# Squares summed on TensorE in the norms, and the query and key norm moved to the two large PSUM tiles, in a two-block transformer kernel

## The chip, the cores and the metric

The kernel runs on one core of a Trainium2 chip. A core has five engines that run side by side and meet at semaphores: PE (TensorE, matrix products into PSUM), DVE (VectorE), ACT (ScalarE), POOL (GpSimd) and SP (SyncE, which here only issues transfers). The metric is device time in microseconds (us) of one execution, the median over the runs. Lower is better.

## The reference, cut to what matters

Two blocks follow each other on 256 tokens of width 1024, all in float32. The first has one layer: stick-breaking attention, a retention branch, and a mixture of 16 experts. The second has two layers, each with half a feed-forward network, a mixing part (neighbourhood attention, pooled means, attention with grouped queries) and another half network, on 256 latent tokens `x` and 256 context tokens `ctx`. The second layer does the context only as far as the latent tokens need it.

```python
def _rmsnorm(x, g):
    y = x32 * lax.rsqrt(jnp.mean(x32 * x32, axis=-1, keepdims=True) + EPS)
    return (y * g.astype(jnp.float32)).astype(x.dtype)
...
h_x = _half_ffn(h_x, norm_g[l, 0], ..., ffn1_up[l], ffn1_down[l])
a_x = _modulate(_rmsnorm(h_x, norm_g[l, 1]), ...)
p_x = a_x @ w_in[l]
q_c = _rope_2d(_rmsnorm(p_x[..., OFF_C_Q:OFF_C_K].reshape(...), q_norm_g[l]), ang_row, ang_col)
k_c = _rope_2d(_rmsnorm(p_x[..., OFF_C_K:OFF_C_V].reshape(...), k_norm_g[l]), ang_row, ang_col)
o_b = _pool_mix(p_x[..., OFF_B_U:OFF_C_Q], pool_w[l], pool_scale[l])
o_c = _gqa_blocks(q_c, ...)
h_x = h_x + mod_x[:, :, 5] * (jnp.concatenate([o_a, o_b, o_c], axis=-1) @ w_out[l])
h_x = _half_ffn(h_x, norm_g[l, 2], ..., ffn2_up[l], ffn2_down[l])
...
return _rmsnorm(h_x, final_g)
```

The change touches two computations: the sum of squares over 1024 features that every `_rmsnorm` needs, and the norm and rotation of the queries and keys, 64 features a head.

## The kernel before, in words

**Products.** Activations lie feature by token: `self.h` holds eight tiles of 128 features by 256 tokens, once for the latent half (`v` = 0) and once for the context half (`v` = 1). A float32 product is made of three (`gemm`, lines 250 to 252): both factors are split into a high and a low part, and high by high, low by high and high by low add up in one PSUM tile. Weights arrive by DMA as `raw`, ACT copies the high part into `w` (L228) and DVE subtracts the low part (L237), for all of the kernel's weights.

**Sum of squares.** A norm's squares are made while the layer before is still writing `h`. `square` takes two feature tiles at once: ACT squares them into a tile `sq`, one engine adds the two halves (L351) and adds the result to `sqa` (L352). That engine is POOL, for the last pair DVE. Where the layer before ends with single tiles (the down projections of the networks), `square1` does the last two feature tiles singly: ACT squares, POOL adds the seventh and DVE the eighth to `sqa` (L357). Then `rstd` sums `sqa` over its 128 partitions by a product with a column of ones, one for each 128 tokens (L323, tile `ss`), DVE makes the reciprocal root of it (`nv`, `nr_y`, L325 and L288 to L303), `spread` turns it into rows again on PE (`rb`, L315), and `apply` multiplies (`xt`, L333) and splits into `xH` and `xL` (L338 and L339), which the next projections read. There are twelve such norms, and each has its two products on PE.

**Queries and keys.** `qk_norm` is a generator, whose steps the mixing part calls between the products of its other projections (`pj`). It waits for three steps, then does five tiles `t`, the keys (4) first and four of queries. For each, `widen` spreads the reciprocal roots (`qrw`, L1543 on ACT, L1545 on DVE for the keys), `scale` transposes them on PE into `qrp` (L1533) and multiplies on DVE (L1535), and a step later `turn` does the rotation: a product `qpp` on PE (L1549), and three DVE operations, of which the first (`qra`, L1551) reads `qpp`. In the first layer a tile has 512 tokens (`full`), in the second 256 for the queries.

**Buffers.** Two rings of PSUM matter. `mm` has four tiles of 128 x 512 and serves the projections `pj`, and before the change `qrp` and `qpp` too. `a2` has two tiles of 128 x 2 x 512, for the attention scores `as` and the sums `qss`. In SBUF, the ring `s` of seven tiles (`s512`) serves `sq`, `xt`, `qrw`, `qra`, and the tiles of `pool_sums` on POOL (`pla`, `plb`, `plc`, `pld`, `py`, L1710 to L1723). A new tile of a ring waits until the last reader of its place is done. A scheduler fixes the order of each engine's instructions when the program is built; each engine then runs its list in order.

**The end.** After the last down projection (`pd`, added into `h` at L698) comes the last norm: `finish` scales `h` by the final gains (L1743), transposes it on PE (`op`, L1747), multiplies by the norm (L1751 on DVE, L1753 on ACT) and stores.

Of the kernel before, what the change touches and what calls it, by code (L numbers as in the profile page):

```python
# [12 lines left out]
ALU = mybir.AluOpType  # L13
# [5 lines left out]
S = 256  # L19
# [151 lines left out]
class Builder:  # L171
# [147 lines left out]
    def rstd(self, sq):  # L319
        nc = self.nc  # L320
        ss = self.nps("ss")
        for t in range(2):
            nc.tensor.matmul(ss[:, t:t + 1], sq[0][:, t * 128:(t + 1) * 128], self.ones[:, 0:1], start=True, stop=True)  # L323
        m = self.small([128, 2], "nv")
        nc.vector.tensor_scalar(m, ss[:, :2], 1.0 / D, EPS, ALU.mult, ALU.add)  # L325
        return self.rsqrt(m, 2, "nr")
# [14 lines left out]
    def square(self, v, i, sq, last=3):  # L341
        nc = self.nc
        t = self.s512("sq")
        hs = self.h[:, 2 * i:2 * i + 2, v * S:(v + 1) * S]
        nc.scalar.activation(t.rearrange("p (j t) -> p j t", j=2), hs, AF.Square)
        e = nc.vector if i == last else nc.gpsimd
        if not sq:
            sq.append(self.scr.tile([128, S], F32, tag="sqa", name="sqa", bufs=2))
            e.tensor_tensor(sq[0], t[:, :S], t[:, S:], ALU.add)
        else:  # L350
            e.tensor_tensor(t[:, :S], t[:, :S], t[:, S:], ALU.add)  # L351
            e.tensor_tensor(sq[0], sq[0], t[:, :S], ALU.add)  # L352

    def square1(self, v, j, sq, e):
        t = self.s512("sq")[:, :S]
        self.nc.scalar.activation(t, self.h[:, j, v * S:(v + 1) * S], AF.Square)
        e.tensor_tensor(sq[0], sq[0], t, ALU.add)  # L357

    def normed(self, l, n, v, sq):
        for _ in range(NORM_LAG[v][0 if n < 2 else 2]):  # L360
# [226 lines left out]
    def ffn(self, l, n, up, dn, vs, side, pace, after):  # L587
        nc = self.nc
        self.raw_n, self.raws = 0, 7
        half = lambda v: slice(v * S, (v + 1) * S)  # L590
        with ExitStack() as st:
# [9 lines left out]
            for pi, nf in enumerate(PARTS):  # L601
# [3 lines left out]
                full = slice(0, N)  # L605
                off_up = OFF_512 if N == 512 else OFF_258 if late else OFF_256
                off_dn = OFF_512 if N == 512 else OFF_256
                for c in range(nf // 2):
# [4 lines left out]
                    for i in range(2):  # L613
# [20 lines left out]
                        for z in range(0, len(todo), 2):  # L634
                            pa, pb = todo[z][1][:, full], todo[z + 1][1][:, full]
                            if late:
                                p = pabs.pop(0)
                                ab = self.small([128, 2], "ab")
                                s = self.s512("fs").rearrange("p (a t) -> p a t", a=2)
# [4 lines left out]
                                t = self.s512("ft")[:, full]  # L644
                                nc.vector.scalar_tensor_tensor(t, s[:, 1], ab[:, 1:2], s[:, 0], ALU.add, ALU.mult)
                            else:
                                s = self.s512("fs")[:, full]
                                nc.scalar.activation(s, pa, AF.Silu)  # L648
                                t = self.s512("ft")[:, full]
# [9 lines left out]
                if pi < len(PARTS) - 1:  # L659
                    for dc in range(4):  # L660
                        v = self.rows(dn, f0 * 128, nf, dc * 256, 256)
                        for i in range(2):
                            w = self.split_w(v[:, :, i * 128:(i + 1) * 128], off_dn)
                            p = self.mm("pd")
                            self.gemm(p[:, full], w, lambda f: hid[f])
                            for v2 in range(N // S):
                                self.residual(p[:, half(v2)], 2 * dc + i, l, n, v2)
                        for _ in range(pace[1] if N == full_n else 1):
                            next(side, None)
                else:  # L670
                    ws = [self.split_w(self.rows(dn, f0 * 128, nf, dc * 256, 256), OFF_256) for dc in range(4)]
                    for v in sorted(vs):
                        sq = []
                        for d in range(KD):
                            cs = slice(d % 2 * 128, d % 2 * 128 + 128)
                            w = [z[:, :, cs] for z in ws[d // 2]]
                            p = self.mm("pd")[:, :S]
                            self.gemm(p, w, lambda f: (hid[f][0][:, half(v)], hid[f][1][:, half(v)]))
                            self.residual(p, d, l, n, v)
                            next(side, None)  # L680
                            self.advance()
                            if d >= 6:
                                self.square1(v, d, sq, nc.vector if d == 7 else nc.gpsimd)
                            elif d % 2:
                                self.square(v, d // 2, sq)
                        for _ in side:
                            pass
                        self.settle()
                        if after is not None:
                            self.pending = self.normed(*after, v, sq)  # L690
                        else:
                            self.sq = sq
# [817 lines left out]
    def qk_norm(self, l, ss, qc, ks, g8, cos, sin, full, P):  # L1510
        nc = self.nc
        kH, kL = ks
        hs = [slice(0, 64), slice(64, 128)]
        NX = 512 if full else 256
        sv = ss[:, :40].rearrange("p (t c a) -> p t c a", t=5, a=2)
        v = P.tile([128, 5, 4, 2], F32, name="qv")
        if not full:
            nc.vector.memset(v, 1.0)
            nc.vector.tensor_scalar(v[:, :4, :2], sv[:, :4, :2], 1.0 / 64, EPS, ALU.mult, ALU.add)
            nc.vector.tensor_scalar(v[:, 4], sv[:, 4], 1.0 / 64, EPS, ALU.mult, ALU.add)  # L1520
        else:
            nc.vector.tensor_scalar(v, sv, 1.0 / 64, EPS, ALU.mult, ALU.add)
        r = self.rsqrt(v.rearrange("p t c a -> p (t c a)"), 40, "qr")
        for _ in range(3):
            yield True
        r = r.rearrange("p (t c a) -> p t c a", t=5, a=2)

        def scale(t):
            n = 512 if t == 4 else NX
            rp = self.mm("qrp")[:, :n]  # L1530
            wide = wides.pop(t)
            for c in range(n // 128):
                nc.tensor.transpose(rp[:, c * 128:(c + 1) * 128], wide[:, c * 128:(c + 1) * 128], self.ident)  # L1533
            g = self.vec("kn", l) if t == 4 else g8
            nc.vector.scalar_tensor_tensor(qc[:, t, :n], qc[:, t, :n], g, rp, ALU.mult, ALU.mult)  # L1535

        def widen(t):
            n = 512 if t == 4 else NX
            wides[t] = self.s512("qrw")[:, :n]
            o = wides[t].rearrange("p (c a d) -> p c a d", a=2, d=64)  # L1540
            i = r[:, t, :n // 128, :, None].to_broadcast([128, n // 128, 2, 64])
            if t < 4:
                nc.scalar.activation(o, i, AF.Copy)  # L1543
            else:
                nc.vector.tensor_copy(o, i)  # L1545

        def turn(t):
            pp = self.mm("qpp")[:, :256]
            nc.tensor.matmul(pp, self.perm2, qc[:, t, :256], start=True, stop=True)  # L1549
            a_ = self.s512("qra")[:, :256]  # L1550
            nc.vector.tensor_tensor(a_, pp, sin, ALU.mult)  # L1551
            nc.vector.tensor_tensor(qc[:, t, :256], qc[:, t, :256], cos, ALU.mult)
            nc.vector.tensor_tensor(qc[:, t, :256], a_, qc[:, t, :256], ALU.add)
            if t == 4:
                for kv in range(2):
                    i = qc[hs[kv], 4, :]
                    for a in range(2):
                        nc.scalar.activation(kH[hs[a], kv, :], i, AF.Copy)
                for kv in range(2):
                    i = qc[hs[kv], 4, :]  # L1560
                    for a in range(2):
                        nc.vector.tensor_tensor(kL[hs[a], kv, :], i, kH[hs[kv], kv, :].bitcast(F32), ALU.subtract)

        last, wides = None, {}
        widen(4)
        widen(0)
        for t in (4, 0, 1, 2, 3, None):
            if t is not None:
                scale(t)
                if t in (4, 0, 1):  # L1570
                    widen((t + 2) % 5 if t < 4 else 1)
                yield True
            if last is not None:
                turn(last)
                yield True
            last = t
# [223 lines left out]
```

## Time and profile before

| | |
|---|---|
| Runs of the kernel before | 2236.61, 2228.87, 2228.74 us; median 2228.87 us |
| The profiled execution | 2224.97 us, with a span of 2223.1 us in the trace |
| PE busy | 2154.5 us, 97% of the span |
| DVE, ACT, POOL busy | 1438.2 us (65%), 816.9 us (37%), 178.0 us (8%) |
| Granted clock of PE, mean | 0.993 of full |

The times of the trace (the rows below) are those of the profiled execution, counted from the start of its span. A start such as 910.30 is a place on that clock. "Idle before" is how long an engine stood before an instruction, and the name behind the arrow is what ended that. A product of float32 operands without the split (as `ss`) shows as two rows of PE in the trace.

### The profile page before, as it was taken

How to read it: one execution, taken by the hardware profiler on the slowest of the kernel's cores; microseconds unless marked ns; L12 is line 12 of the kernel's file. 1: busy time of each engine (PE TensorE's matmuls, PEld its weight loads, DVE VectorE, ACT ScalarE, POOL GpSimd, SP SyncE). 2: the span in 40 equal slices, each digit the busy share in tenths (PEclk: the TensorE clock that was granted, in tenths of full speed). 3: DMA queues.
4: the chain of work that ended last, by engine and by line, in shares of the span. 5: the costliest groups of instructions: out<-in, count | busy, mean ns of one | idle time of the engine just before them, and what ended most of it. 6: DMA issues, size and time to landing. Idle time of an engine off the chain costs nothing.

```text
span 2223.1 us, 32479 instructions
## 1 busy us (share of the span) xinstructions
PE 2154.5 (97%) x13295; PEld 1775.8 (80%) x13295; DVE 1438.2 (65%) x2516; ACT 816.9 (37%) x1256; POOL 178.0 (8%) x204
## 2 busy tenths in 40 slices
PE   8999999997999999989999999999999999999998
PEld 8789975543688888977888877788878888879998
DVE  5656852221489787766678777638874345877776
ACT  5564531110233322347642222224222223575443
POOL 0200100000000000340120000000000003312000
PEclk9999999999999999999999999999999999999999
DMA  8674769998946655320236555333553212317551
GB/s 260 209 259 127 253 246 336 374 384 352 352 153 217 231 181 165 87 67 29 95 118 204 185 181 189 128 125 115 197 185 104 90 58 78 109 34 234 185 181 47
DMA packets 285461, 395.91 MB, mean 178 GB/s; under 512 B 18156, under 2 KB 220540, under 8 KB 285180
## 3 DMA queue, kind: packets, MB, share of 16 engines
q1 hardware_dynamic: 284288, 392.33, 52.2%
q8 instruction: 106, 1.74, 0.3%
q0 software_dynamic: 576, 1.18, 0.2%
q14 instruction: 47, 0.39, 0.1%
q10 hardware_dynamic: 444, 0.27, 0.0%
HBM read 392.71 MB, written 1.05 MB: 177 GB/s over the span
## 4 chain that ended last, share of the span: by engine, by line
PE 68%; DVE 6%; ACT 1%; POOL 1%; issue 1%; ACTq 0%; DVEq 0%; POOLq 0%
PE pab L250 12%; PE pab L251 12%; PE pab L252 12%; PE pd L250 6%; PE pd L251 6%; PE pd L252 6%; PE pj L250 1%; PE pj L251 1%; PE pj L252 1%; PE egu L1162 1%; PE aT L1652 1%; PE as L1623 1%; PE ao L1669 1%; DVE w L237 1%; PE ada_ps L531 1%; PE po L250 1%
## 5 line engine op out<-in xcount | busy, mean ns | idle before, releaser
L228 ACT ACTIVATE w<-raw 128x1024 fp32r<-128x1024 f32 (+2 forms) x432 | 425.5, 990 | 664.6 <-PE pd L252 238.6
L237 DVE TENSOR_TENSOR w<-raw,w 128x1024 fp32r<-128x1024 f32 (+2 forms) x422 | 481.2, 1150 | 181.3 <-ACT w L228 179.4
L251 PE MATMUL pab<-xL,w 128*128 128x512 f32 (+2 forms) x1600 | 545.0, 341 | 2.6 <-DVE xL L339 1.6
L250 PE MATMUL pab<-xH,w 128*128 128x512 f32 (+2 forms) x1600 | 545.2, 341 | 0.2
L252 PE MATMUL pab<-xH,w 128*128 128x512 f32 (+2 forms) x1600 | 544.1, 341 | 0.0
L250 PEld LDWEIGHTS pab<-xH,w 128*128 128x128 f32 x1600 | 301.7, 189 | 48.8 <-issue 8.2
L251 PEld LDWEIGHTS pab<-xL,w 128*128 128x128 f32 x1600 | 301.8, 189 | 42.3 <-issue 4.1
L252 PEld LDWEIGHTS pab<-xH,w 128*128 128x128 f32 x1600 | 301.8, 189 | 37.9 <-issue 4.1
L549 DVE SCALAR_TENSOR_TENSOR acc<-raw,sT,acc 128x512 f32<-128x512 f32 x420 | 284.8, 745 | 0.0
L250 PE MATMUL pd<-hH,w 128*128 128x512 f32 (+1 forms) x800 | 264.9, 333 | 0.5 <-ACT hH L241 0.2
L251 PE MATMUL pd<-hL,w 128*128 128x512 f32 (+1 forms) x800 | 264.5, 332 | 0.0
L252 PE MATMUL pd<-hH,w 128*128 128x512 f32 (+1 forms) x800 | 264.0, 331 | 0.0
L250 PE MATMUL pj<-xH,w 128*128 128x256 f32 (+1 forms) x816 | 248.5, 306 | 10.9 <-DVE qra L1551 5.2
L251 PE MATMUL pj<-xL,w 128*128 128x256 f32 (+1 forms) x816 | 243.3, 298 | 1.4 <-DVE xL L339 0.5
L252 PE MATMUL pj<-xH,w 128*128 128x256 f32 (+1 forms) x816 | 242.6, 298 | 0.5 <-DVE w L237 0.5
L250 PEld LDWEIGHTS pj<-xH,w 128*128 128x128 f32 x816 | 155.3, 191 | 26.5 <-DVE qra L1551 6.0
L250 PEld LDWEIGHTS pd<-hH,w 128*128 128x128 f32 x800 | 149.6, 188 | 20.4 <-ACT fs L648 3.4
L698 DVE SCALAR_TENSOR_TENSOR h<-pd,gmod,h 128x256 f32<-128x256 f32 x224 | 100.7, 478 | 99.0 <-PE pd L252 98.6
L252 PEld LDWEIGHTS pd<-hH,w 128*128 128x128 f32 x800 | 150.0, 188 | 16.8 <-issue 1.7
L251 PEld LDWEIGHTS pd<-hL,w 128*128 128x128 f32 x800 | 150.4, 188 | 15.4 <-DVE hL L242 0.3
L251 PEld LDWEIGHTS pj<-xL,w 128*128 128x128 f32 x816 | 155.7, 191 | 7.1 <-DVE xL L339 1.9
L252 PEld LDWEIGHTS pj<-xH,w 128*128 128x128 f32 x816 | 155.5, 191 | 5.5 <-DVE w L237 0.8
(388 smaller groups left out, 2457.5 us busy)
## 6 DMA issues: line engine op xcount, KB each, us to landing
raw<-ffn_up SPq DMA_DIRECT2D x94, 1024.0 KB, 5.3
raw<-w_ada SPq DMA_DIRECT2D x72, 1024.0 KB, 5.3
raw<-ffn_down SPq DMA_DIRECT2D x52, 768.0 KB, 4.7
raw<-w_in SPq DMA_DIRECT2D x32, 1024.0 KB, 5.7
raw<-w_exp_gate SPq DMA_DIRECT2D x32, 1024.0 KB, 10.0
raw<-w_exp_up SPq DMA_DIRECT2D x32, 1024.0 KB, 9.7
raw<-w_exp_down SPq DMA_DIRECT2D x32, 1024.0 KB, 8.7
raw<-w_gate SPq DMA_DIRECT2D x8, 1024.0 KB, 5.6
```

What stands on the lines that cost most here:

```text
L228: self.nc.scalar.activation(wh, v, AF.Copy)
L237: self.nc.vector.tensor_tensor(wl, v, wh.bitcast(F32), ALU.subtract)
L250: mm(o, wH[:, k, :], aH, start=(first and k == 0), stop=False)
L251: mm(o, wH[:, k, :], aL, start=False, stop=False)
L252: mm(o, wL[:, k, :], aH, start=False, stop=(last and k == n - 1))
L531: mm(ps[g * 32:(g + 1) * 32, :], self.unit[:, 31 - r:63 - r], acc[v], start=(u < 2), stop=(u > 3))
L549: ins = V.scalar_tensor_tensor(acc[v], w[:, g, :], s, acc[v], ALU.mult, ALU.add)
L698: self.nc.vector.scalar_tensor_tensor(hs, p, self.gmod[:, l, n, d, v:v + 1], hs, ALU.mult, ALU.add)
L1162: mm(pr[a * 64:a * 64 + 64, m, :], xg[p // 2][:, q * 2 + kk, es[a] % 4 * 64:es[a] % 4 * 64 + 64], w[:, a, kk * 512:(kk + 1) * 512], start= ...
L1623: mm(o[:, c], qs, x[i][:, c], start=(i == 0 and not (near and c.start == 0)), stop=(i == 1))
L1652: nc.tensor.transpose(T[:, j * 128:(j + 1) * 128], e[:, a, j * 128:(j + 1) * 128], self.ident)
L1669: mm(o[hs[a], qt * 128:(qt + 1) * 128], v[:, j, vo[a]:vo[a] + 64], pT[:, a, j, :], start=(j == 0), stop=(j == 3))
```

## The change

The diff, whole:

```diff
@@ rstd
         for t in range(2):
-            nc.tensor.matmul(ss[:, t:t + 1], sq[0][:, t * 128:(t + 1) * 128], self.ones[:, 0:1], start=True, stop=True)
+            for i, s in enumerate(sq):
+                nc.tensor.matmul(ss[:, t:t + 1], s[:, t * 128:(t + 1) * 128], self.ones[:, 0:1],
+                                 start=(i == 0), stop=(i == len(sq) - 1))
@@ square
-        e = nc.vector if i == last else nc.gpsimd
-        if not sq:
+        e = nc.gpsimd
+        if i == last:
+            sq.extend((t[:, :S], t[:, S:]))
+        elif not sq:
             sq.append(self.scr.tile([128, S], F32, tag="sqa", name="sqa", bufs=2))
             e.tensor_tensor(sq[0], t[:, :S], t[:, S:], ALU.add)
         else:
             e.tensor_tensor(t[:, :S], t[:, :S], t[:, S:], ALU.add)
             e.tensor_tensor(sq[0], sq[0], t[:, :S], ALU.add)
 
-    def square1(self, v, j, sq, e):
+    def square1(self, v, j, sq):
         t = self.s512("sq")[:, :S]
         self.nc.scalar.activation(t, self.h[:, j, v * S:(v + 1) * S], AF.Square)
-        e.tensor_tensor(sq[0], sq[0], t, ALU.add)
+        sq.append(t)
@@ ffn
-                                self.square1(v, d, sq, nc.vector if d == 7 else nc.gpsimd)
+                                self.square1(v, d, sq)
@@ qk_norm
-        for _ in range(3):
+        for _ in range(3 if full else 5):
             yield True
@@ scale
             n = 512 if t == 4 else NX
-            rp = self.mm("qrp")[:, :n]
+            both[t] = self.a2("qrp")
+            rp = both[t][:, 0, :n]
@@ turn
-            pp = self.mm("qpp")[:, :256]
+            pp = both.pop(t)[:, 1, :256]
@@ qk_norm
-        last, wides = None, {}
+        last, wides, both = None, {}, {}
```

In words: the last two squared feature tiles of a norm are no longer added to `sqa`, and `ss` is the sum of three products for each 128 tokens in place of one. In the program built from it PE has 48 matrix products more (12 norms by 4), DVE 17 additions fewer and POOL 7 fewer. The query and key norm's two PSUM tiles are now the two halves of one tile of the ring `a2`, and in the second layer it begins two steps later.

The scheduler orders the instructions anew. Three places, with the rows of each engine's order. `sqc` also names the constant that holds the ones and the identity. What stands in brackets is what the instruction may have to wait for; line numbers beyond L320 are one to five higher after the change.

On PE at the program's end, from the last down projection to the last transposes, before:

```order
L252 MATMUL pd<-hH,w 128x256
L323 MATMUL ss<-sqc,sqa 128x1 [waits DVE_49]
L323 MATMUL ss<-sqc,sqa 128x1
L1747 MATMUL op<-sqc,h 128x128 x11
L1747 MATMUL op<-sqc,h 128x128 [waits DVE_49] x2
L1747 MATMUL op<-sqc,h 128x128 x3
```

and after:

```order
L252 MATMUL pd<-hH,w 128x256
L324 MATMUL ss<-sqc,sqa 128x1 [waits DVE_49,Pool_49]
L324 MATMUL ss<-sqc,sq 128x1 [waits Activation_49]
L1752 MATMUL op<-sqc,h 128x128 [waits DVE_49]
L1752 MATMUL op<-sqc,h 128x128 x3
L1752 MATMUL op<-sqc,h 128x128 [waits DVE_49]
L1752 MATMUL op<-sqc,h 128x128 x3
L1752 MATMUL op<-sqc,h 128x128 [waits DVE_49]
L324 MATMUL ss<-sqc,sq 128x1 [waits Activation_49]
L324 MATMUL ss<-sqc,sqa 128x1
L324 MATMUL ss<-sqc,sq 128x1 x2
```

Two products of the sum and nine transposes of `op` have moved ahead of the product that reads the last square.

On DVE in the second layer's query and key norm, from the last step of its reciprocal root to the rotation of the keys, before:

```order
L237 TENSOR_TENSOR w<-raw,w 128x1024 [waits DMAHW1_49,PE_49,Activation_49]
L308 SCALAR_TENSOR_TENSOR qr_y<-qr_a,qr_y 128x40 [waits DVE_49]
L1545 COPY qrw<-qr_y 128x512 [waits DVE_49]
L1535 SCALAR_TENSOR_TENSOR qc<-qc,vT,qrp 128x512 [waits PE_49]
L1535 SCALAR_TENSOR_TENSOR qc<-qc,g_16744,qrp 128x256 [waits PE_49]
L237 TENSOR_TENSOR w<-raw,w 128x1024 [waits Activation_49]
L1551 TENSOR_TENSOR qra<-qpp,rot_16707 128x256 [waits DMASW6_49,PE_49,Pool_49]
```

and after:

```order
L237 TENSOR_TENSOR w<-raw,w 128x1024 [waits DMAHW1_49,PE_49,Activation_49]
L308 SCALAR_TENSOR_TENSOR qr_y<-qr_a,qr_y 128x40 [waits DVE_49]
L237 TENSOR_TENSOR w<-raw,w 128x1024 [waits PE_49,Activation_49]
L1550 COPY qrw<-qr_y 128x512 [waits DVE_49,Pool_49]
L1540 SCALAR_TENSOR_TENSOR qc<-qc,vT,qrp 128x512 [waits PE_49]
L1540 SCALAR_TENSOR_TENSOR qc<-qc,g_16755,qrp 128x256 [waits PE_49]
L237 TENSOR_TENSOR w<-raw,w 128x1024 [waits DMAHW2_49,Activation_49]
L1556 TENSOR_TENSOR qra<-qrp,rot_16718 128x256 [waits DMASW6_49,PE_49,Pool_49]
```

One split of weights more (L237) now stands ahead of `qrw`, and `qrw` itself waits for POOL, whose tiles of `pool_sums` have taken the places of the ring `s` ahead of it. On PE the first `qrp` of this layer stands 25 rows of `pj` later than before.

On PE around the wait of the first layer's query and key norm, the rows from the product `qpp` of the third query tile, before:

```order
L1549 MATMUL qpp<-qc,sqc 128x256 [waits DVE_49] x2
L250 MATMUL pj<-xH,w 128x512 [waits DVE_49]
L251 MATMUL pj<-xL,w 128x512
L252 MATMUL pj<-xH,w 128x512
L250 MATMUL pj<-xH,w 128x512
```

and after:

```order
L1554 MATMUL qrp<-qc,sqc 128x256 [waits DVE_49]
L250 MATMUL pj<-xH,w 128x512
L251 MATMUL pj<-xL,w 128x512
L1538 MATMUL qrp<-sqc,qrw 128x128 [waits DVE_49,PE_49,Activation_49]
L1538 MATMUL qrp<-sqc,qrw 128x128 x3
L252 MATMUL pj<-xH,w 128x512
```

Before, the projection `pj` waits for the first reader of a `qpp`. After, two rows of the projection go ahead, and the last `scale` (tile 3) waits instead, for the reader of the `a2` tile that it takes over, which is the `qra` of tile 1. Until then `scale` of tile 3 stood ahead of the wait, now it stands behind it.

## Rows read from the trace of the kernel before

**Rows 1.** The page, part 1: busy us, share of the span, instructions.
```profile
PE 2154.5 (97%) x13295; PEld 1775.8 (80%) x13295; DVE 1438.2 (65%) x2516; ACT 816.9 (37%) x1256; POOL 178.0 (8%) x204
```

**Rows 2.** The page, part 4: the chain that ended last, by engine.
```profile
PE 68%; DVE 6%; ACT 1%; POOL 1%; issue 1%; ACTq 0%; DVEq 0%; POOLq 0%
```

**Rows 3.** The waits of PE: waited for, us in total, times, longest.
```profile
PE pj L250 <- DVE qra L1551: 5.2, 2, 3.4
...
PE ss L323 <- DVE sqa L357: 4.0, 1, 4.0
...
PE qrp L1533 <- DVE qrw L1545: 2.0, 1, 2.0
PE rb L315 <- DVE nr_y L303: 1.9, 4, 0.6
PE pab L251 <- DVE xL L339: 1.6, 5, 0.6
...
PE ss L323 <- DVE sqa L352: 0.8, 1, 0.8
PE pj L250 <- DVE qc L1535: 0.8, 1, 0.8
```

**Rows 4.** The tile `ss`: count, ns min/median/max, first and last start, form.
```profile
L323 PE MATMUL ss<-sqc,sqa x48: 164/250/372, 262.7 to 2214.7; 128*128 128x1 f32 x48
```

**Rows 5.** Timeline of PE around one `ss`: start us, us, line, operation.
```profile
910.30 0.50 PE L323 MATMUL ss<-sqc,sqa 128*128 128x1 f32 x4
910.66 0.36 PE L250 MATMUL pd<-hH,w 128*128 128x256 f32 x1
910.86 0.28 PE L251 MATMUL pd<-hL,w 128*128 128x256 f32 x1
910.98 0.28 PE L252 MATMUL pd<-hH,w 128*128 128x256 f32 x1
```

**Rows 6.** Groups of DVE by line: busy us, mean ns, idle before.
```profile
L357 DVE TENSOR_TENSOR sqa<-sqa,sq 128x256 f32<-128x256 f32 x7 | 2.9, 420 | 2.5 <-ACT sq L356 2.5
```

**Rows 7.** Timeline of DVE, first layer's query and key norm.
```profile
982.82 0.73 DVE L1535 SCALAR_TENSOR_TENSOR qc<-qc,g,qrp 128x512 f32<-128x512 f32 x1
...
987.19 0.42 DVE L1551 TENSOR_TENSOR qra<-qpp,rot 128x256 f32<-128x256 f32 x1 [1.42 <-POOL py L1722]
```

**Rows 8.** Timeline of PE, the same place.
```profile
987.67 0.50 PE L250 MATMUL pj<-xH,w 128*128 128x512 f32 x1 [3.36 <-DVE qra L1551]
...
992.12 0.40 PE L1623 MATMUL as<-kH,qs 128*128 128x512 f32 x1
992.35 0.39 PE L1623 MATMUL as<-kL,qs 128*128 128x512 f32 x1
...
999.60 0.38 PE L1623 MATMUL as<-kH,qs 128*128 128x256 f32 x1 [2.74 <-ACT e L1634]
```

**Rows 9.** Windows: us; busy of PE, PEld, DVE, ACT, POOL; granted clock; DMA.
```profile
990.00:1000.00 10.00, 7.26 (x30) 5.62 (x29) 9.46 (x12) 2.67 (x6) 9.69 (x12) 0.92 0.01 2
...
2210.00:2223.00 13.00, 4.62 (x21) 4.13 (x20) 6.46 (x24) 2.21 (x4) 1.88 (x3) 0.64 0.22 81
```

**Rows 10.** Timeline of DVE, second layer's query and key norm.
```profile
1913.78 0.20 DVE L308 SCALAR_TENSOR_TENSOR qr_y<-qr_a,qr_y 128x40 f32<-128x40 f32 x1
...
1916.33 0.71 DVE L308 SCALAR_TENSOR_TENSOR qr_y<-qr_a,qr_y 128x40 f32<-128x40 f32 x1
...
1919.87 1.55 DVE L237 TENSOR_TENSOR w<-raw,w 128x1024 fp32r<-128x1024 f32 x1
1922.66 0.42 DVE L1551 TENSOR_TENSOR qra<-qpp,rot 128x256 f32<-128x256 f32 x1 [1.24 <-POOL plc L1716]
```

**Rows 11.** Timeline of PE at the end.
```profile
2214.05 1.01 PE L323 MATMUL ss<-sqc,sqa 128*128 128x1 f32 x4 [3.96 <-DVE sqa L357]
2214.93 3.65 PE L1747 MATMUL op<-sqc,h 128*128 128x128 f32 x16
```

**Rows 12.** Timeline of DVE at the end.
```profile
2218.62 0.75 DVE L1751 TENSOR_SCALAR ot<-op,nr_y 128x512 f32<-128x512 f32 x1 [0.74 <-PE op L1747]
```

## The prediction, made before the changed kernel had run

> **What bounds the kernel now.** The page comes first. PE is busy 2154.5 of 2223.1 us, DVE 65%, POOL 8% [rows 1], and in the chain that ended last PE holds 68% and DVE 6%, no other engine more than 1% [rows 2]. So work taken from DVE or POOL gains only where PE waits for it, and work given to PE costs its whole time, except where PE waits anyway. The second view is therefore the list of PE's waits. Those that the change can reach are few: for `qra` 5.2 us, for the last addition of squares (L357) 4.0 in one place and (L352) 0.8, for `qrw` 2.0, for `nr_y` 1.9, for `xL` 1.6, for the first reader of a `qrp` 0.8 [rows 3]. Together they are 16.3 us, 0.7% of the time. That is the most that the edits could win, and no more than 0.5% (11.1 us), above or below, counts as the same time, about what a measurement of this kernel can tell from no change.
>
> **The added products.** The trace has 48 rows for 24 products of `ss` [rows 4], two for each. In a dense stretch four rows take 910.66 - 910.30 = 0.36 us to the next start, 0.09 a row; but the first `pd` behind them then holds the next up for 0.20 in place of the usual 0.12 (910.86 to 910.98) [rows 5], which belongs to them: 0.44 for four, 0.11 a row. Each norm gets four products, eight rows, 0.89 us. Eleven norms lie in dense stretches: 11 x 0.89 = **9.8 us gross**; the twelfth is the tail. Lower bound by the 0.09: 7.9.
>
> The Trainium skill (TensorE: Matmul & The Clock Gate, Back-to-back issue gap) puts a product with so few moving columns at about 25 ns; by it the 88 rows would be 2.2 us and this term 7.6 us less. The rows above disagree, and the page's section LDWEIGHTS, 107 ns for 128 columns of weights, is nearer to them: here each product loads a tile of squares as its weights for one moving column.
>
> **The removed additions.** An addition on DVE takes 0.42 us [rows 6], 17 of them 7.1 us. DVE isn't the bound, so most of this is cover. It comes back only in the stretches after a norm's sum, where DVE has a queue of `apply` and PE waits for it: `nr_y` 1.9, `xL` 1.6, and the 0.8 before the mixture of experts, where `ss` itself waits for L352; 4.3 us in all [rows 3]. In those stretches PE is late by its own extra rows, which also eats waits. All 4.3 back would leave +5.5, none of it +9.8. The 0.8 should go whole; of the 3.5 others I take nearly all, 3.1, since the added rows of a norm's second half (`v` = 1) and the shorter DVE queue both fall into the waits of the first: 9.8 - 0.8 - 3.1 = **+5.9**. Range +3.6 (the 7.9 less all of the 4.3) to +9.8. POOL's seven additions count as nothing: they lie under the last products of `pd`, and POOL has 1% of the chain [rows 2]; if that cover were gone, one would be worth at least DVE's 0.42, 2.9 for the seven.
>
> **The first layer's query and key norm.** PE waits 0.8 for `qc` because `pj` needs the place of a `qrp` [rows 3]; this goes. The long wait of 3.36 [rows 8] is another matter. `pj` waits there for `qra`, at 987.19, but DVE had itself stood 1.42 us for POOL's `py` [rows 7], whose tile held a place of the ring `s`. The edit doesn't touch that ring. In the order after, two rows of `pj` go ahead (0.46 us, 0.23 each by the rows at 992.12 [rows 8]), and then `scale` of tile 3 waits for the same `qra`, since five `a2` tiles pass through two places. So the wait moves to another instruction and keeps some 2.9 of 3.36. What is late next: the DVE half of `scale`, 0.73 us, stood at 982.82 ahead of the wait [rows 7] and now stands behind it, in a stretch in which DVE is busy 9.46 of 10 us [rows 9], and the second group of scores, at 999.60, waited for ACT behind that queue [rows 8]. And `scale` of tile 2 must wait for the `qra` of tile 0, which I put at about 1 us, between 0 and 1.5, by the 0.8 that it replaces. Sum: -0.8 - 0.5 (the two rows) + 0.7 (the moved DVE step) + 0.7 (its four transposes, at the 0.23 that a row of `op` takes at the lower clock [rows 11], less what the scores leave free) + 1.0 = **+1.1**, range -2.8 (the 0.8 and the whole 3.4 gone, the two moved steps left) to +2 (the new wait 1.5, `scale` in full).
>
> **The second layer's.** The first `qrp` waits 2.0 for `qrw`, and a `pj` then waits 5.2 - 3.4 = 1.8 for `qra` [rows 3]. Twenty-five rows of `pj` now go ahead, 25 x 0.11 = 2.8 us, more than the 2.0. But DVE's steps there are stretched while POOL works (L308 0.20 and then 0.71 us), and `qra` at 1922.66 stood 1.24 us for POOL's `plc` [rows 10]. In the new order `qrw` needs a place that `pool_sums` holds, and a split of weights (L237, 1.55 us) moves between. By these rows the first `qra` ends 1.55 (the split) to 2.8 us (the split and POOL's 1.24 once more) later than before; I take 1.8, since ACT, which widens the queries, waits for POOL too and can run ahead in part. Of the 25 rows' 2.8 us, 2.0 cover the first wait and 0.8 are left: the second becomes 1.8 - 0.8 + 1.8 = 2.8, where the two were 3.8: **-1.0**, range -3.8 (both gone) to +2 (2.8 late, no cover left, and 1.24 for POOL at a second tile: 1.8 + 2.8 + 1.2 = 5.8).
>
> **The tail.** After the last `pd`, PE stands 3.96 us for the addition L357, its granted clock then is at the lower level of 1.2 GHz (a mean of 0.64 over the last 13 us is 9.4 us at 0.5), `ss` takes 0.88 to the next start, and 16 rows of `op` 3.65 [rows 9, 11]. Without the addition `ss` starts 0.42 us earlier [rows 6]; but eight rows stand behind the last square and not four, 0.9 us at the full and 1.8 at the lower level. Nine transposes go ahead, so that the 0.74 that DVE stood for `op` [rows 12] goes. -0.42 - 0.74 + 0.9 at the lower level is -0.3; -0.42 - 0.74 and nothing for the rows at the full level is -1.2; I take **-0.8**, range -1.3 to +0.4.
>
> **Sum.** 5.9 + 1.1 - 1.0 - 0.8 = +5.2 us. On the profiled execution, 2224.97, this makes 2230.2; that execution lies 3.9 below the median of the runs, 2228.87, from which the sum would give 2234.1. The runs of before differ by more than this, and I start from the middle of the two, 2226.9: 2232.
>
> **Rivals.**
> 1. *The two big tiles do free PE.* If the wait for POOL were not binding, 3.36 and 0.8 of the first layer go, 1.7 more since its 12 rows of `pj` take 4.45 us from 987.67 to 992.12 [rows 8] at the lower level in place of 2.75, and 3.8 of the second, with -1.2 in the tail: +5.5 - 4.2 - 1.7 - 3.8 - 1.2 = -5.4, some 2221. For it: `pj` loses no bank to `qrp`. Against it: the 1.42 and 1.24 for POOL [rows 7, 10].
> 2. *Slower: the ring of two holds PE once more.* One mechanism: every `scale` from the third on waits for a `qra`, which waits for POOL. If each layer gets one more wait as long as those it has, 3.36 and 2.0 [rows 3, 8], and DVE gives nothing back at the norms, +9.8 + 5.4 = +15.2, 2242. It decides once these waits pass 1.3 us beyond the gross 9.8. The Trainium skill (GPSIMD Engine Reference, Specifications) says that GpSimd shares its SBUF interfaces with VectorE for operations with two inputs there; L308's 0.71 against 0.20 agrees, and the moved DVE steps stand in that company.
> 3. *The move at the query and key norm does nothing*: waits change their names, and the norms and the tail alone count, +5.1, 2232 too; it is told apart by the waits, not by the time.
> 4. *The short price for small products* (25 ns by the page above): 5.2 - 7.6 = -2.4, 2224 or 2225. The rows of `ss` speak against it.
>
> **How the numbers follow.** Forecast 0.55, rival 3 0.15, rival 1 0.15, rival 2 0.12, rival 4 0.03. All but rival 2 lie within 11.1 us of before; of rival 1 a quarter could pass -11.1 if the norms return more too (0.04), and of rival 2 three quarters pass +11.1 (0.09). Faster 0.04, same 0.87, slower 0.09. The range takes in rival 1 and the lower half of rival 2: 2220 to 2241; the forecast's own is 2226 to 2238.
>
> **What the profile after would show.** `ss` with 144 rows, eight rows more in 0.9 us at each dense norm (wrong if the next `pd` starts 0.56 or less behind the first row). The 4.0 us for L357 gone, in its place short waits of `ss` for ACT. A wait of PE `qrp` for DVE `qra` of some 3 us near 985, in place of that of `pj`, with the DVE row still behind POOL; if it is under 1 us, rival 1 holds. In the second layer the 2.0 for `qrw` gone and about 2 to 3 us for `qra`; if above 4, rival 2. I am wrong at the root if PE's busy time grows by less than 5 us, or if a place elsewhere, such as the experts, whose order the scheduler changed too, moves by more than 2 us.

## The result, and the profile after

The changed kernel takes 2241.83 us (median of 13 runs, 2240.05 to 2251.17), the kernel before 2230.14 us (13 runs, 2226.75 to 2239.72). The ratio is 1.0058 with a 95% interval of 1.0044 to 1.0071: **slower by 12.9 us** (9.8 to 15.8), just past the 0.5% that was set as the bound of "the same", though the interval still reaches below it. (The 12.9 comes from the ratio; the medians lie 11.7 apart.) The prediction was 2232 with 2220 to 2241, and 0.09 for slower.

PE's busy time grew by 13.6 us, and its share of the span stayed at 97%. Page, part 1, of the changed kernel:

```profile
PE 2168.1 (97%) x13391; PEld 1792.0 (80%) x13391; DVE 1434.2 (64%) x2499; ACT 818.4 (37%) x1256; POOL 170.6 (8%) x197
```

PE's waits in the changed kernel (waited for, us in total, times, longest), beside [rows 3]:

```profile
PE qrp L1538 <- DVE qra L1556: 7.8, 3, 5.1
...
PE ss L324 <- POOL sqa L356: 4.0, 3, 2.3
...
PE pab L251 <- DVE xL L341: 1.1, 3, 0.6
...
PE qrp L1538 <- ACT qrw L1548: 1.0, 1, 1.0
PE qrp L1538 <- DVE qrw L1550: 1.0, 1, 1.0
...
PE ss L324 <- ACT sq L360: 0.7, 1, 0.7
...
PE rb L315 <- DVE nr_y L303: 0.4, 1, 0.4
```

The 4.0 for the last addition on DVE are gone, and 4.0 for an addition on POOL have come. The waits for `qra` grew from 5.2 to 7.8, those for `nr_y` and `xL` fell from 3.5 to 1.5. The sum of these waits hardly moved (16.0 here, 16.3 in [rows 3]), so the loss isn't in their sum. What follows finds it in the added rows, in two waits that stand at other places than before, and in stretches at the lower clock behind them.

Where it lies is read from the starts of the same product in both traces: the n-th `pab`, `pd` or `pj` of one shape against the n-th of the other. A step in the difference is time lost in that stretch. The table has these steps in us, each from medians over the products of a stretch. The two profiled executions are 15.1 apart in all, of which 3.0 lie before 900 us. Those 3.0 are not used: in the traces of five other kernels of this document, whose work up to there is that of the kernel before, the same products also lie 0.6 to 6.2 later than in its trace.

| Stretch of the kernel | after minus before |
|---|---|
| four pairs of norms in the networks (910, 1130, 1505, 1880 us) | +1.0 +1.1 +0.3 +0.9 = +3.3 |
| first layer's query and key norm and attention | +1.8 |
| second layer's | +0.3 |
| late norm of the second layer (2030 us) | **+5.9** |
| tail | +0.8 |

The steps are differences of single traces, so where the clock happens to fall in one of them counts too.

**The added rows** stand as they were priced. The timeline of PE at the first of these norms, after:

```profile
913.28 0.28 PE L324 MATMUL ss<-sqc,sqa 128*128 128x1 f32 x2
913.42 0.58 PE L324 MATMUL ss<-sqc,sq 128*128 128x1 f32 x4
913.87 0.36 PE L324 MATMUL ss<-sqc,sqa 128*128 128x1 f32 x2
914.09 0.58 PE L324 MATMUL ss<-sqc,sq 128*128 128x1 f32 x4
914.54 0.36 PE L250 MATMUL pd<-hH,w 128*128 128x256 f32 x1
```

Twelve rows take 1.26 us to the next `pd`, four took 0.36 [rows 5]: 0.90 more for the eight added ones, where 0.89 was forecast.

**The late norm.** PE's timeline before (one row), then after, then a row of POOL's after:

```profile
2028.43 0.50 PE L323 MATMUL ss<-sqc,sqa 128*128 128x1 f32 x4
```

```profile
2032.24 0.28 PE L251 MATMUL pab<-xL,w 128*128 128x258 f32 x1
2034.79 0.38 PE L324 MATMUL ss<-sqc,sqa 128*128 128x1 f32 x2 [2.27 <-POOL sqa L356]
2035.03 0.36 PE L252 MATMUL pab<-xH,w 128*128 128x258 f32 x1
...
2037.44 0.85 PE L324 MATMUL ss<-sqc,sq 128*128 128x1 f32 x4
2038.15 0.57 PE L324 MATMUL ss<-sqc,sqa 128*128 128x1 f32 x2
2038.57 0.99 PE L324 MATMUL ss<-sqc,sq 128*128 128x1 f32 x4
2039.43 0.56 PE L251 MATMUL pab<-xL,w 128*128 128x258 f32 x1
```
```profile
2033.15 1.59 POOL L356 TENSOR_TENSOR sqa<-sqa,sq 128x256 f32<-128x256 f32 x1
```

One product of the sum (two rows) stands alone, ahead of the others and of fourteen rows of `pab`, and waits 2.27 us for POOL. The order on PE shows why. Before, both products stand together behind the `pab`; after, the first has moved ahead, since it needs `sqa` and no longer the last square. After:

```
10524 L251 MATMUL pab<-xL,w 128x258
10525 L324 MATMUL ss<-sqc,sqa 128x1 [waits Pool_49]
10526 L252 MATMUL pab<-xH,w 128x258
...
10539 L250 MATMUL pab<-xH,w 128x258
10540 L324 MATMUL ss<-sqc,sq 128x1 [waits Activation_49]
```

Everything of PE is queued behind that one product (the numbers are places in PE's list). Products of the sum stand ahead of the others at six more norms of the order after, the tail among them. PE waits for them at two of the six only: 0.64 us at 1141 us, and in the tail.

What follows the wait at the late norm runs slower too. From 2036 on the rows of `pab` start 0.21 us apart where 0.12 is usual. The granted clock (the last column but two), in windows of 10 us (the tail's 13), is below full in stretches where it was full before, and lower in the first layer and the tail than in [rows 9]. One window of before at the late norm, then those of after:

```profile
2030.00:2040.00 10.00, 9.95 (x83) 9.75 (x83) 8.89 (x29) 6.63 (x8) 0.00 (x0) 1.00 1.10 349
```

```profile
990.00:1000.00 10.00, 6.53 (x21) 5.39 (x22) 6.34 (x10) 2.54 (x3) 9.46 (x14) 0.66 0.01 2
1930.00:1940.00 10.00, 10.00 (x51) 8.86 (x50) 7.61 (x11) 6.09 (x11) 9.77 (x11) 0.83 0.07 26
2030.00:2040.00 10.00, 7.22 (x39) 6.60 (x40) 5.38 (x10) 2.49 (x4) 4.58 (x5) 0.80 0.95 309
2040.00:2050.00 10.00, 10.00 (x75) 10.00 (x75) 7.51 (x26) 6.11 (x7) 0.00 (x0) 0.86 0.77 244
2225.00:2238.00 13.00, 5.64 (x28) 5.15 (x28) 5.36 (x22) 2.10 (x4) 0.46 (x1) 0.58 0.22 81
```

At the late norm (0.20 + 0.14) x 10 / 0.5 = 6.8 us ran at the lower level of 1.2 GHz, which is worth half of it, 3.4 us, on a PE that is dense there. With the wait of 2.3 and the rows of 0.9 this is 6.6; 5.9 were lost.

**The first layer's query and key norm**, DVE and PE after, beside [rows 7, 8]:

```profile
992.90 0.42 DVE L1556 TENSOR_TENSOR qra<-qrp,rot 128x256 f32<-128x256 f32 x1 [3.40 <-POOL plb L1717]
```
```profile
993.47 1.09 PE L1538 MATMUL qrp<-sqc,qrw 128*128 128x128 f32 x4 [5.15 <-DVE qra L1556]
```

`qra` waits for POOL as before, but for a later tile of it (`plb`, not `py`): 3.40 where it was 1.42. The place that it takes in the ring has moved.

**The tail**, PE and DVE after, beside [rows 11, 12]:

```profile
2224.12 0.28 PE L252 MATMUL pd<-hH,w 128*128 128x256 f32 x1
2225.51 0.38 PE L324 MATMUL ss<-sqc,sqa 128*128 128x1 f32 x2 [1.11 <-POOL sqa L356]
2226.56 0.38 PE L324 MATMUL ss<-sqc,sq 128*128 128x1 f32 x2 [0.67 <-ACT sq L360]
2226.80 1.92 PE L1752 MATMUL op<-sqc,h 128*128 128x128 f32 x9
2228.51 0.42 PE L324 MATMUL ss<-sqc,sq 128*128 128x1 f32 x2
2228.80 0.56 PE L324 MATMUL ss<-sqc,sqa 128*128 128x1 f32 x2
2229.23 0.99 PE L324 MATMUL ss<-sqc,sq 128*128 128x1 f32 x4
```
```profile
2227.84 0.35 DVE L1748 TENSOR_SCALAR h<-h,vT 128x256 f32<-128x256 f32 x1 [0.55 <-ACT sq L360]
2230.26 0.16 DVE L327 TENSOR_SCALAR nv<-ss 128x2 f32<-128x2 f32 x1 [2.06 <-PE ss L324]
```

The last square is there at 2227.8 (DVE's wait for it ends then), but PE is still at the nine transposes, at the lower clock, until 2228.5, and the eight rows behind it take 1.75. `nv` comes 2230.26 - 2224.12 = 6.14 us after the last `pd` starts; before it came 5.3 after. From that `pd` to the end of the span it is 14.1 us here and 13.3 before. How much of this is the tail's own is taken up at the run of the late norm below.

### The profile page after: what moved, and what is told of

Same layout as the page of the kernel before. It is cut to its first block, busy times and chain, and to the rows that moved or that the text cites. A ratio compares the mean times of both kernels' runs of the same rounds, so it can differ in the third digit from the quotient of the medians.

```text
span 2238.2 us, 32636 instructions
## 1 busy us (share of the span) xinstructions
PE 2168.1 (97%) x13391; PEld 1792.0 (80%) x13391; DVE 1434.2 (64%) x2499; ACT 818.4 (37%) x1256; POOL 170.6 (8%) x197
## 3 DMA queue, kind: packets, MB, share of 16 engines
q8 instruction: 107, 1.75, 0.3%
HBM read 392.71 MB, written 1.05 MB: 176 GB/s over the span
## 4 chain that ended last, share of the span: by engine, by line
PE 68%; DVE 4%; POOL 2%; issue 1%; ACT 1%; DVEq 0%; POOLq 0%; ACTq 0%
PE pab L250 12%; PE pab L252 12%; PE pab L251 12%; PE pd L250 6%; PE pd L251 6%; PE pd L252 6%; PE egu L1166 1%; PE aT L1657 1%; PE pj L250 1%; PE pj L251 1%; PE pj L252 1%; PE ao L1674 1%; PE as L1628 1%; PE po L250 1%; PE ada_ps L535 1%
## 5 line engine op out<-in xcount | busy, mean ns | idle before, releaser
L237 DVE TENSOR_TENSOR w<-raw,w 128x1024 fp32r<-128x1024 f32 (+2 forms) x422 | 480.7, 1150 | 190.9 <-ACT w L228 189.0
```

The costliest lines, as they stand in the source:

```text
L237: self.nc.vector.tensor_tensor(wl, v, wh.bitcast(F32), ALU.subtract)
```

## The experiments

Every ratio is to the kernel before on the same chip, with its 95% interval.

**The norms alone**: the diff's `rstd`, `square` and `square1`, with `qk_norm` as before.

> The norms' part alone (squares summed on PE), the query and key norm as before. Theory A (the norms carry the loss: by the offsets of the two traces +3.4 around the experts, +3.1 in the four pairs of norms, +5.5 at the late norm, +0.8 in the tail): 11 to 13 us above before, with the 2.3 us wait of ss for POOL at the late norm and half the clock behind it still there. Theory B (the two big tiles carry it): 3 us above before or less.

1.0059 (1.0035 to 1.0083): 13 us, the whole loss. Its trace has the wait of 2.3 us for POOL at the late norm and loses 5.1 us there.

**The query and key norm alone**: the other half of the diff.

> The query and key norm's part alone (big tiles, five steps in the second layer), the norms as before. Theory A: 2 to 3 us above before (first layer +1.8, second +0.4), within the noise. Theory B: 9 us above or more.

1.0005 (0.9991 to 1.0018): 1 us, not to be told from none. In its trace the first layer loses 1.8 and the second 0.3, as in the whole change, and `qra` waits 3.40 for `plb` there too: the longer wait comes from the big tiles, not from the norms.

**The order of the three products turned round**, on the norms alone:

```diff
-            for i, s in enumerate(sq):
+            for i, s in enumerate(reversed(sq)):
```

> The norms' part alone, with the three products in reverse order, the last square first and sqa last, so that no product of a sum can be ordered ahead of the last square. Theory A1 (a product put early that waits for POOL, and the lower clock that follows, is half of the norms' loss): 4 to 6 us faster than the norms' part in the old order, and no wait of ss for POOL at the late norm. Theory A2 (the added rows are the loss, the wait is covered by work that waits later): the same time as the norms' part, within 2 us.

1.0037 (1.0021 to 1.0053): 8 us above before, 5 below the norms in the old order. The intervals of the two overlap. No product of a sum stands alone any more. The late norm costs 0.7 in this trace. The four pairs of norms cost 3.9, where three traces in the old order have 3.3 (the changed kernel), 2.9 (the late norm alone turned round, below) and 4.6 (the norms alone): there the order makes no difference that single traces show. The pair of 910 us costs 1.9, and behind it the clock falls in this trace (0.83 from 930 to 940 us), which it doesn't in the others.

**The added products alone**: a column of zeros in a tile of its own, used for two products more for each 128 tokens.

```diff
+        self.zero = self.const.tile([128, 1], F32, name="zero")
+        nc.vector.memset(self.zero, 0.0)
...
-            nc.tensor.matmul(ss[:, t:t + 1], sq[0][:, t * 128:(t + 1) * 128], self.ones[:, 0:1], start=True, stop=True)
+            for i in range(3):
+                nc.tensor.matmul(ss[:, t:t + 1], sq[0][:, t * 128:(t + 1) * 128],
+                                 (self.zero if i else self.ones)[:, 0:1], start=(i == 0), stop=(i == 2))
```

> The kernel before with two products more for each 128 tokens, of sqa with a column of zeros: the same 48 products added, no addition removed, nothing that can go early. Price of the rows alone: by 0.11 us a row 9.8 us above before, if PE's waits behind the norms absorb nothing; by the theory that a later PE eats waits for xL and nr_y, 5 to 7; by a short price of 25 ns a product 1 to 2.

1.0162 (1.0136 to 1.0187): 36 us, more than any of the three prices. The difference to the trace before grows steadily through the networks, where no `ss` stands, so the run doesn't price the products. Two runs took it apart.

**The added products with the zeros of an old constant** (`self.before`, whose first column is zero, in place of `self.zero`):

> The kernel before with two products more for each 128 tokens, of sqa with a column of zeros that an old constant already holds, so that no tile lies elsewhere in memory: the price of the 48 products alone. The run before this one put its zeros into a tile of their own and came out 36 us slower, spread evenly over all of the networks' products, which the 48 cannot do. If the place of the tiles made that, the drift in the networks is gone here and 5 to 10 us above before are left, some 0.9 at each norm. If the products themselves made it, it comes again.

1.0041 (1.0027 to 1.0056): 9 us. One norm of it, on PE, and its waits:

```profile
918.20 1.40 PE L324 MATMUL ss<-sqc,sqa 128*128 128x1 f32 x12
919.46 0.37 PE L250 MATMUL pd<-hH,w 128*128 128x256 f32 x1
```
```profile
PE pab L251 <- DVE xL L341: 1.3, 4, 0.6
PE rb L315 <- DVE nr_y L303: 0.9, 2, 0.5
```

The same 1.26 us for twelve rows, and the waits for `xL` and `nr_y` fall from 3.5 to 2.2 although no addition is removed: a later PE eats part of them by itself. In the four pairs of the networks this kernel loses 1.3, 1.0, 0.9 and 1.8, together 5.0, against 3.3 with the additions removed.

**The tile of zeros alone**, with nothing that reads it:

> The kernel before with a constant tile of one column of zeros that nothing reads, so that the tiles behind it lie elsewhere in memory; no product added. If the place of the tiles made the drift of the first run of the added products: about 27 us above before (36 less the 9 that the 48 products cost with the old constant), spread over the networks' products. If not: the same as before.

1.0093 (1.0078 to 1.0109): 21 us, for a tile of four bytes a partition, where 27 were expected. With the 9 us of the products this makes 30 of the 36; 6 stay open. It is taken up below.

**The late norm alone turned round**, all else as in the changed kernel:

```diff
-        r = self.rstd(self.sq)
+        r = self.rstd(self.sq[::-1])
```

> The changed kernel, with the order of the three products reversed at one norm only, the late one of the second layer. Theory A1 (the early product that waits 2.4 us for POOL, and the lower clock behind it, make the 5.5 us there): the late norm costs about 1 us, and the time is 4 to 5 us below the changed kernel's, 7 to 8 above before. Rival (the waits only move, since what follows the norm is bound elsewhere): no faster than the changed kernel by more than 2.

1.0030 (1.0017 to 1.0043), 2236.8 us: 5 below the changed kernel. The two intervals just part (1.0044 is the lower end of the change). Its late norm, PE's timeline and the windows:

```profile
2033.88 0.50 PE L324 MATMUL ss<-sqc,sq 128*128 128x1 f32 x4
2034.62 0.38 PE L324 MATMUL ss<-sqc,sqa 128*128 128x1 f32 x2 [0.24 <-POOL sqa L356]
2034.86 0.58 PE L324 MATMUL ss<-sqc,sq 128*128 128x1 f32 x4
```
```profile
2020.00:2030.00 10.00, 9.50 (x79) 9.09 (x78) 8.21 (x16) 7.36 (x13) 6.66 (x9) 1.00 0.44 145
2030.00:2040.00 10.00, 9.25 (x75) 8.75 (x75) 8.34 (x25) 4.03 (x6) 4.41 (x5) 1.00 0.97 315
```

POOL ends as late as in the changed kernel, the products stand behind `pab` and wait 0.24, and the clock is full. The stretch loses 0.6. The four traces agree on the clock: where the early product waits (the changed kernel, the norms alone) it is low for 6.8 us behind it, and with the order turned (here, the norms turned round) it stays full there. In all the two profiled executions are 6.7 apart, and 1.3 of this lie in the tail, which the edit doesn't touch: its rows stand in the same order, after the same waits.

```profile
2218.68 0.28 PE L252 MATMUL pd<-hH,w 128*128 128x256 f32 x1
2221.36 1.18 PE L1752 MATMUL op<-sqc,h 128*128 128x128 f32 x9
2222.41 0.38 PE L324 MATMUL ss<-sqc,sq 128*128 128x1 f32 x2
```

Here the clock falls 4.8 us after the last `pd` starts, in the changed kernel after 3.0 (before, after 3.8). The nine transposes take 1.05 us to the next start where they took 1.71, and the tail from that `pd` to the end 12.8 us, 0.5 less than before. Seven traces with the tail of before (the first one and six of the other runs) have 12.8 to 13.3, and the three with the changed tail 12.8 (here), 13.8 (the norms alone) and 14.1 (the changed kernel).

**POOL in fewer tiles.** In `pool_sums` the third and fourth partial sums are written over the first and second, the same operations in the same order:

```diff
-                    w3 = self.s512("plc")
+                    w3 = w
-                    w4 = self.s512("pld")
+                    w4 = w2
```

On the query and key norm alone, and on the kernel before as control:

> The query and key norm's part alone, with the pooled means on POOL in two tiles fewer for each of the four-step sums (in place, the same operations), so that qra and qrw find places in the ring of seven earlier. If the long waits of PE for qra stand behind POOL's tiles: the 5.2 us wait of the first layer falls under 2, and the time is 4 to 6 us below the part alone, 2 to 5 below before. If DVE's own queue sets them: no change of the waits, the same time as before.

> The kernel before with the same saving of tiles on POOL, nothing else changed: the control for the run with the big tiles. If POOL's tiles hold PE through the ring: the 3.4 us wait of pj for qra shrinks by 2 or more, 2 to 4 us faster. If not: the same.

0.9990 (0.9978 to 1.0003) and 0.9994 (0.9981 to 1.0007): neither can be told from before. The waits moved, as PE's lists and one row of DVE show, first with the big tiles, then in the control:

```profile
PE qrp L1534 <- DVE qra L1552: 8.1, 4, 2.8
```
```profile
987.31 0.42 DVE L1552 TENSOR_TENSOR qra<-qrp,rot 128x256 f32<-128x256 f32 x1 [0.62 <-POOL py L1723]
```
```profile
PE as L1623 <- ACT e L1634: 4.1, 2, 3.8
...
PE pj L250 <- DVE qra L1551: 2.7, 2, 1.9
```

With fewer tiles on POOL the `qra` that stood 3.40 for POOL with the big tiles alone stands 0.62. The longest wait of PE for it falls from 5.2 to 2.8, not under 2 as expected, and the total stays (8.1 for 7.8). In the control 2.5 of the 5.2 are gone, and the scores take 1.0 back by a longer wait for ACT.

**Which layer.** The saving with the big tiles and three steps in the second layer, and with the big tiles in the first layer alone:

```diff
-        for _ in range(3 if full else 5):
+        for _ in range(3):
...
+            both[t] = self.a2("qrp") if full else None
+            rp = (both[t][:, 0, :] if full else self.mm("qrp"))[:, :n]
...
```

> The query and key norm in the big tiles with the saving of tiles on POOL, but with three steps ahead of it in the second layer as before the change. If the two further steps are what loses in the second layer (by the trace the part gains 1.8 in the first layer and gives 1 back in the second): 1 to 3 us below before. If the big tiles lose there: the same as before or above.

> The saving of tiles on POOL, and the big tiles in the first layer's query and key norm only, the second layer as before the change. If the first layer's 1.8 us is real and nothing takes it back: 2 us below before, the best of the versions; a gain under 0.1 per cent cannot be told from none.

1.0008 (0.9997 to 1.0019) and **0.9982 (0.9971 to 0.9993)**, 2227.06 us. The two further steps are not the loss in the second layer: with three, the big tiles lose 5.7 us there by the trace, where with five they lost 0.3. The steps make up for the tiles, by the traces; the intervals of the runs with three and with five still touch. The last kernel is the one that beats both, by 0.2% over the one before: its first layer gains 2.5 by the trace and nothing takes it back, and the squares stay as they were. The control gains 1.2 in the same place, and the intervals of the two overlap, so what the big tiles add to the saving on POOL isn't shown.

## Why the prediction missed

**The step that failed is the late norm.** The prediction charged "Eleven norms lie in dense stretches: 11 x 0.89", the late norm as one of them, as if the added rows always stood behind the old ones. It measured 5.9 in place of 0.89. For the tail the prediction says that products go ahead of the last square; at the late norm the same had happened, and it doesn't mention it. There the first product moved ahead of the work that had hidden POOL, and waits for it. The prediction's sentence that "POOL's seven additions count as nothing" is about the removed ones, which no run prices; POOL's last remaining addition (1.59 us beside DVE's split of weights, 0.75 in the median) had become what that product waits for. With the order turned round at this one place the wait and the fall of the clock are gone and the runs are 5 us quicker, which makes the change +0.3%. Of the 9.8 us between 2232 and 2241.83 the late norm is thus 5.0, and the base (below) 3.2.

**The tail** had the right parts, and its sign is open. Forecast was -0.8 at a clock between the levels, range -1.3 to +0.4. The changed kernel's trace has +0.8, with the lower clock from 3.0 us after the last `pd` on; the trace with the late norm turned round has -0.5 with the same order of the tail and a clock that falls later. The addition and DVE's wait for `op` went as forecast. What was left out is that the nine transposes that moved ahead stand in the way of the last square, 0.7 us at the lower clock and under 0.1 at the full one, and that the four stores are issued one after the other at the end: SP takes 2.00 us for them before and 1.83 after, from the first finished tile on, so that DVE's 0.74 doesn't come back in full.

**The rows and the removed additions.** The rows were sized rightly: 0.90 was measured for a norm's eight. In the four pairs of norms 3.3 of 8 x 0.89 = 7.1 us were lost, so 3.8 came back, where 3.1 was taken for all dense norms together. The reason given was half right: the waits for `xL` and `nr_y` fall mostly because PE comes later, with the additions kept too. What the removed additions are worth is little. Over the four pairs 5.0 are lost with the additions kept, and 3.3, 2.9 and 4.6 in three traces without them. At the last pair the clock falls in the first and the last of these four traces and not in the others; over the first three pairs, where it falls in none, it is 3.3 with the additions and 2.4, 2.4 and 2.8 without, within the noise of the runs.

**The first layer's query and key norm** lost 1.8, +1.1 was forecast. That the wait moves to `scale` of tile 3 was right, that it keeps 2.9 of 3.36 was not: `qra` now waits for a later tile of POOL, and the wait became 5.15. **The second layer's** lost 0.3, -1.0 was forecast; the waits came to 1.0 + 1.0 + 1.1 = 3.1, forecast 2.8, and 3.4 us at the lower clock were not foreseen. Both together stay within the noise, as the run of this half alone shows, so rival 1 (the big tiles free PE) and rival 2 (the ring holds PE by more than 5 us) are both out as sums. The mechanism of rival 2 did occur, for 2.6 us more of waiting for `qra`. That its 2242 is the measured time is luck: its 5.4 us of new waits aren't there, and the loss is at the norms. What rival 3 says of this move holds for the time (1.0005). Rival 4 is out by the 0.90 for eight rows.

**The base** was chosen 3.2 us too low. With more runs the median of before is 2230.1, not the 2226.9 between its profiled execution and the first three runs. Against 2230 the forecast would have been 2235 and the range would have ended at 2244, so it would have held the measured time with the late norm still mis-priced in it.

The sum by the steps: forecast +5.9 + 1.1 - 1.0 - 0.8 = +5.2; by the trace +3.3 (pairs) + 5.9 (late) + 1.8 + 0.3 + 0.8 = +12.1, against 12.9 by the runs. The two norms of the first block and the experts, which the prediction named as a sign of being wrong at the root, can't be read from single traces (3.0 here, among 0.6 to 6.2 in kernels that leave them alone) and are left open. PE's busy time, its other sign, grew by 13.6 and not by less than 5.

## What to carry to other kernels

A sum that is split so that its parts are ready at different times gives the scheduler a part to put early. On an engine that runs its list in order, that part brings its own wait along, and everything behind it pays. So after such an edit look at every place where a part now stands ahead, not at one (here seven, of which the late norm cost most), and ask what had hidden the producer that it waits for. Where waiting early gains nothing, order the parts so that the last one to be ready comes first: it gave 5 us at the late norm here, and nothing that could be seen at the pairs. When a wait of PE goes away in one list and returns in another, compare the granted clock of the two stretches before calling it even.

## What the hardware showed that was not expected

A constant tile of one column of float32, read by nothing, made the kernel 0.93% slower (0.78 to 1.09%). It moves the tiles that are allocated after it. The traces have each engine's instructions in the same order as before, but for the one DVE instruction at the start that writes the zeros, so the order isn't the cause. PE's products of `pab` with 512 columns start 0.233 us apart in a stretch (six steps from 1189.75 to 1191.15) where 0.227 was (six from 1179.77 to 1181.13), and over all 864 of one line the mean row is 397 ns for 391, while those of `pd` with 512 columns keep their 391. Before, then with the tile:

```profile
L250 PE MATMUL pab<-xH,w 128*128 128x512 f32 x864 | 337.8, 391 | 0.0
L250 PE MATMUL pab<-xH,w 128*128 128x512 f32 x864 | 343.2, 397 | 0.0
```

That the place of the tiles does it is what is left, not what was tried; which of the moved tiles it would be wasn't tried either. But an experiment that adds a tile, however small, needs a control that adds the tile alone: here it hid a cost of 9 us behind one of 21.
